# The first feed-forward of a two-layer decoder: seven column blocks accumulated chunk by chunk in whole fp32 products instead of four in split products

## Chip, cores and metric

One NeuronCore of a Trainium2 chip. The metric is the device time of one execution in microseconds. The program is fully unrolled; five engines (PE, DVE, ACT, POOL and SP as DMA queue) work through fixed instruction lists and wait for each other by semaphores.

## Reference

Two decoder layers on 256 tokens of width 1024, every sub-layer with an RMS norm and a shift, scale and gate from the conditioning c. Only the very first sub-layer matters here:

```python
c_act = jax.nn.silu(c)
mod = (c_act @ w_ada[l] + b_ada[l]).reshape(bsz, 3, 3, D_MODEL)
sh, sc, gt = _ada(mod, 0)
h = h + 0.5 * gt * swiglu(modulate(rms_norm(h, norm_g[l, 0]), sh, sc), ffn_w_in[l, 0], ffn_w_out[l, 0])
...
def modulate(x, shift, scale): return x * (1.0 + scale) + shift
def swiglu(x, w_in, w_out):
    g, u = jnp.split(x @ w_in, 2, axis=-1)
    return (jax.nn.silu(g) * u) @ w_out
```

w_in is 1024 x 5632, so x @ w_in has 22 pairs of 128-column blocks (a gate block and an up block); w_out is 2816 x 1024. Everything is float32.

## The kernel before

Activations lie transposed: 8 chunks of 128 features by 256 tokens. An fp32 product is made of three fp32r products (`mm3`, L466 to L468): both operands are split into a high part (a cast to fp32r) and a low part (the rest). A weight block of 1 MB ("w": one pair of column blocks, two halves of 128x1024) goes from HBM into one of four `st` buffers; ACT casts each half to `wh` (L384 or L387) and DVE subtracts to get `wl` (L413). Two of these subtractions, the fourth and the fifth that the program emits (`NLP = [4, 5]` in `low`), are given to POOL. The first eight halves lie in pieces of 512 columns in tiles of the pool `y` (`EX1 = 8`), later ones in `wh` and `wl`. "Sum" below means one such pair of column blocks: two halves x 8 chunks x 3 products = 48 matmuls of 256 columns into one PSUM bank. The first feed-forward's first product has 22 sums.

The conditioning is made by DVE: a block "a" of 1 MB (w_ada) holds shift and scale of one chunk, and two multiply-and-reduce instructions (L393) turn it into two columns of `mod`. `first_input` has a closure `each(k)`: it emits block a of chunk k, the two small DVE operations on it, and on ACT the chunk `uh[k]` = high part and `v` = the whole value in fp32; POOL makes the low part `ul[k]` from the two (L1650) and the next normed chunk (L1631).

So the first feed-forward cannot start before its conditioning. `ORD` says in which order the first blocks are loaded and used: a at an "a", a weight block at a "w". In `ffn`, at an "a" the chunk is applied to all weight halves that are there, at a "w" the new halves are applied to all chunks that are there. The first four sums grow that way. Then `prepare(NPREP)` gets four more halves ready, `act(j)` turns each finished bank into `silu(g) * u` and splits it (ACT L737, DVE L738, ACT L275, DVE L276), `tables()` loads rope tables and gains and lets POOL multiply them out (L1672 to L1692, 39 instructions), and the remaining 18 sums follow one by one. Their halves, and the a blocks of the later sub-layers between them, are emitted by `fill`, which is called from `clk.tick` and asks a planner's clock what would be on time. All of this fixes the order of each engine's list when the program is built; `pin` keeps it.

Of the kernel before, what the change touches and what calls it, by code (L numbers as in the profile page):

```python
# [29 lines left out]
NT = 6  # L30
ORD = 'aaaawawawwaa'
NLP = [4, 5]
# [29 lines left out]
NPREP = 4  # L62
UPTO = 21, 26, 40, 52, 60, 68, 76
P = 128
D = 1024
KC = 8
S = 256
# [156 lines left out]
class _Kernel:  # L224
# [55 lines left out]
    def plan(self):  # L280

        io = self.io
        q = []
# [12 lines left out]
        ffn_in = lambda n: blk("w_in", n * NJ, NJ)  # L296
        ffn_out = lambda n: blk("w_out", n * 11, 11)
        U = UPTO
        ws = ffn_in(0)
        nw = 0  # L300
        for e in ORD:
            q.append(("a", len(q) - nw) if e == "a" else ("w",) + ws[nw])
            nw += e == "w"
        phase(ws[nw:], U[0])
        phase(ffn_out(0), U[1])
        ws = []
# [8 lines left out]
        ws = ffn_in(2)  # L315
# [10 lines left out]
        for j, e in enumerate(q):  # L326
            if j == nsa:
                self.stop = len(self.queue)
            for i in range(2):
                if e[0] == "a" or i * 1024 < e[2]:  # L330
                    self.queue.append((e, i))
# [4 lines left out]
        self.released, self.hold = 0, False  # L336
        self.freed = []
        self.lows = []
        self.lpos, self.issued, self.staged, self.stages = 0, 0, {}, 4
        self.depth, self.slack, self.lag = 6, SG, 0.0  # L340

    def load(self, upto=None):

        clk, sync = self.clk, self.nc.sync
        while self.lpos < len(self.queue) and (upto is None or self.lpos < upto):
            e, i = self.queue[self.lpos]
# [15 lines left out]
            if e[0] == "w":  # L362
                sync.dma_start(out=st[:, 0:e[2]], in_=e[1])
            else:
                sync.dma_start(out=st, in_=self.io["w_ada"][e[1]])
            for _ in range(1 if e[0] == "w" and e[2] == 1024 else 2):
                self.staged[self.lpos] = st, clk.dma + 2000
                self.lpos += 1

    def emit(self):  # L370
# [4 lines left out]
        self.qpos += 1  # L375
        clk = self.clk
        early = e[0] == "a" and e[1] < EARLY
        src = self.st if early else self.st[:, i * 1024:(i + 1) * 1024]
# [344 lines left out]
    def ffn(self, u, gate_fn, prep, each=None):  # L723
# [35 lines left out]
        if each is not None:  # L759
            ks = 0  # L760
            for e in ORD:
                if e == "a":
                    each(ks)
                    if w:
                        outer(ks, range(len(w)))
                    ks += 1
                else:
                    ps.append(self.psmm() if len(ps) < 3 else self.pssc())
                    n = len(w)
                    w += [self.half(n + i > 0) for i in range(2)]  # L770
                    for k in range(ks):
                        outer(k, range(n, n + 2))
            first = len(ps)
        else:
# [9 lines left out]
            for k in range(K1, KC):  # L784
                outer(k, range(2 * first))
        if each is not None:
            self.prepare(NPREP)
        for j in range(first):
            act(j0 + j, ps[j])
        if each is not None:  # L790
            self.tables()
# [824 lines left out]
    def first_input(self):  # L1616
# [7 lines left out]
        nc.scalar.copy(out=rstd, in_=self.rstd)  # L1624
        hn = []

        def norm():
# [9 lines left out]
        def each(k):  # L1637
# [7 lines left out]
            T = clk.on("V", 200)  # L1645
            v = self.tmp((P, S))
            for o in (th[:, k, :], v):
                nc.scalar.activation(out=o, in_=hn[k], func=AF.Identity, bias=sh[:, k:k + 1], scale=gs[:, k:k + 1])
                T = clk.A(2 * S, T)
# [141 lines left out]
def _layout(i):  # L1791
# [18 lines left out]
    wi = i["ffn_w_in"].reshape(4, KC, P, 2, NJ, P).transpose(0, 4, 2, 3, 1, 5)  # L1810
    L["w_in"] = ct(wi).reshape(4 * NJ, P, 2048)
    wo = i["ffn_w_out"].reshape(4, NJ, P, KC, P).transpose(0, 3, 1, 2, 4).reshape(4 * 11, 16, P, P)
    L["w_out"] = ct(wo.transpose(0, 2, 1, 3)).reshape(44, P, 2048)
# [46 lines left out]
```

## Time and profile before

| | |
|---|---|
| time before, median of 3 runs | 1305.77 us (1304.62 to 1307.18) |
| the profiled execution | 1304.5 us; its span 1302.7 us |
| busy in the span | PE 94%, DVE 75%, ACT 50%, POOL 20% |
| first matmul of the first feed-forward | at 24.30 us |
| its first four sums done, next sum starts | 60.37 us |
| first matmul with w_out | 163.18 us |

In the trace every fp32r matmul is one record of MATMUL and one of LDWEIGHTS (row PEld); a plain fp32 matmul leaves two of each. Records of PE overlap, so the distance of starts is the pace and the length of a record is not. PEclk in the views is 1.00 where the throttle granted the full rate; whether TensorE runs at 1.2 or 2.4 GHz is seen from the distance of starts.

### The profile page before, as it was taken

Reading aid. Unit: us, or ns where it says so; the run is one execution under the profiler, and the core shown is the slowest. Engines: PE = TensorE matmul, PEld = TensorE weight load, DVE = VectorE, ACT = ScalarE, POOL = GpSimd, SP = SyncE. Lnnn points to the kernel's source line nnn. Section 1 sums busy time; section 2 is a strip of 40 time slices with the busy share of each in tenths; the row PEclk is TensorE's granted clock in tenths of the full one; section 3 lists DMA queues with packets and bytes.
Section 4 is the critical chain, followed back from the end, with each engine's and each line's share of the span. In section 5 each row is a group of like instructions: output and inputs, shape, how many; then the busy total and the mean of one; then the engine's idle time right before and its main releaser. Section 6 shows DMA issues by size and latency. Waiting matters only on the chain.

```text
span 1302.7 us, 23375 instructions
## 1 busy us (share of the span) xinstructions
PE 1224.2 (94%) x9373; PEld 1146.2 (88%) x9373; DVE 976.3 (75%) x1743; ACT 646.3 (50%) x1126; POOL 255.3 (20%) x356
## 2 busy tenths in 40 slices
PE   4899999789989898899999999999999889999998
PEld 3899999677777687799999999989998778999998
DVE  6788886866768677578888878878778997766652
ACT  4545554434445444456545446545435477654441
POOL 3460010462433525110000100030001353000000
PEclk9999999989999999899999999999999899999999
DMA  8889877534353544245888956776983003466650
GB/s 324 303 300 341 325 302 280 196 148 173 133 203 148 197 134 163 91 163 206 327 321 320 343 208 242 272 276 244 334 311 142 33 2 132 162 257 227 239 198 17
DMA packets 42733, 284.50 MB, mean 218 GB/s; under 512 B 5249, under 2 KB 6273, under 8 KB 9346
## 3 DMA queue, kind: packets, MB, share of 16 engines
q1 hardware_dynamic: 42626, 283.02, 58.8%
q8 instruction: 73, 1.20, 0.4%
q14 instruction: 34, 0.28, 0.1%
HBM read 281.96 MB, written 1.05 MB: 217 GB/s over the span
## 4 chain that ended last, share of the span: by engine, by line
PE 73%; DVE 13%; POOL 8%; ACT 3%; issue 2%; DMA 0%; SPq 0%; ACTq 0%; DVEq 0%; POOLq 0%
PE mm L466 18%; PE mm L467 18%; PE mm L468 18%; PE mm L849 3%; PE mm L850 3%; PE mm L851 3%; DVE wl L413 2%; PE tp L906 2%; POOL y L938 2%; POOL rs_t L581 2%; POOL rs_t L584 2%; POOL rs_y L586 2%; POOL rs_t L585 1%; DVE y L1455 1%; DVE st L393 1%
## 5 line engine op out<-in xcount | busy, mean ns | idle before, releaser
L413 DVE TENSOR_TENSOR wl<-st,wh 128x1024 fp32r<-128x1024 f32 x361 | 436.3, 1234 | 94.4 <-ACT wh L387 94.0
L387 ACT CAST wh<-st 128x1024 fp32r<-128x1024 f32 x361 | 369.4, 1048 | 137.3 <-PE mm L468 45.3
L466 PE MATMUL mm<-uh,wh 128*128 128x256 f32 x1304 | 366.5, 281 | 1.6 <-DVE y L738 1.6
L467 PE MATMUL mm<-uh,wl 128*128 128x256 f32 x1304 | 367.9, 282 | 0.0
L468 PE MATMUL mm<-ul,wh 128*128 128x256 f32 x1304 | 365.0, 280 | 0.0
L468 PEld LDWEIGHTS mm<-ul,wh 128*128 128x128 f32 x1304 | 246.8, 189 | 0.0
L466 PEld LDWEIGHTS mm<-uh,wh 128*128 128x128 f32 x1304 | 244.5, 187 | 1.9 <-DVE y L738 1.8
L467 PEld LDWEIGHTS mm<-uh,wl 128*128 128x128 f32 x1304 | 245.0, 188 | 0.0
L466 PE MATMUL mm<-y,wh 128*128 128x256 f32 x832 | 233.4, 281 | 0.1
L467 PE MATMUL mm<-y,wl 128*128 128x256 f32 x832 | 232.4, 279 | 0.0
L468 PE MATMUL mm<-y,wh 128*128 128x256 f32 x832 | 232.2, 279 | 0.0
L393 DVE CUSTOM_DVE_ANT_0 st<-st,cact 128x1024 f32<-128x1024 f32 x152 | 186.7, 1258 | 0.0
L466 PEld LDWEIGHTS mm<-y,wh 128*128 128x128 f32 x832 | 156.4, 188 | 1.1 <-issue 0.9
L467 PEld LDWEIGHTS mm<-y,wl 128*128 128x128 f32 x832 | 156.4, 188 | 0.0
L468 PEld LDWEIGHTS mm<-y,wh 128*128 128x128 f32 x832 | 156.4, 188 | 0.0
L849 PE MATMUL mm<-wh,uh 128*128 128x512 f32 (+1 forms) x336 | 135.0, 402 | 0.0
L850 PE MATMUL mm<-wl,uh 128*128 128x512 f32 (+1 forms) x336 | 131.0, 390 | 0.1
L851 PE MATMUL mm<-wh,ul 128*128 128x512 f32 (+1 forms) x336 | 130.3, 388 | 0.0
L524 POOL TENSOR_TENSOR y<-y 128x256 f32<-128x256 f32 x20 | 22.8, 1138 | 360.3 <-ACT y L505 360.3
L895 POOL TENSOR_TENSOR y<-y 128x512 f32<-128x512 f32 (+1 forms) x26 | 32.3, 1251 | 265.4 <-DVE y L894 157.5
L737 ACT ACTIVATE y<-mm 128x256 f32<-128x256 f32 x84 | 32.2, 383 | 94.2 <-PE mm L468 94.0
L849 PEld LDWEIGHTS mm<-wh,uh 128*128 128x128 f32 x336 | 66.3, 197 | 14.1 <-issue 1.2
(254 smaller groups left out, 1659.2 us busy)
## 6 DMA issues: line engine op xcount, KB each, us to landing
st<-w_in SPq DMA_DIRECT2D x88, 1024.0 KB, 5.1
st<-w_ada SPq DMA_DIRECT2D x76, 1024.0 KB, 5.7
st<-w_out SPq DMA_DIRECT2D x44, 1024.0 KB, 6.8
st<-w_qk SPq DMA_DIRECT2D x24, 1024.0 KB, 4.8
st<-w_va SPq DMA_DIRECT2D x8, 1024.0 KB, 4.7
st<-w_o SPq DMA_DIRECT2D x8, 1024.0 KB, 4.8
st<-w_vb SPq DMA_DIRECT2D x4, 1024.0 KB, 5.0
st<-w_q SPq DMA_DIRECT2D x4, 1024.0 KB, 6.8
```

The lines of the kernel that those rows point to most:

```text
L387: nc.scalar.copy(out=wh, in_=src)
L393: nc.vector.tensor_tensor_reduce(out=src, in0=src, in1=self.cact, scale=1.0, scalar=0.0, op0=ALU.mult, op1=ALU.add, accum_out=self.mod[:, ...
L413: (self.nc.gpsimd if eng == "G" else self.nc.vector).tensor_tensor(out=o, in0=src[:, c], in1=i.bitcast(F32), op=ALU.subtract)
L466: mm(out=out, lhsT=ah, rhs=bh, start=start, stop=False, **kw)
L467: mm(out=out, lhsT=al, rhs=bh, start=False, stop=False, **kw)
L468: mm(out=out, lhsT=ah, rhs=bl, start=False, stop=stop, **kw)
L581: eng.tensor_tensor(out=t, in0=y, in1=y, op=ALU.mult)
L737: nc.scalar.activation(out=sg, in_=ps[:, 0:S], func=AF.Silu)
L849: mm(out=ps[tt], lhsT=uh[k][:, c], rhs=wh[:, o], start=k == 0, stop=False)
L850: mm(out=ps[tt], lhsT=uh[k][:, c], rhs=wl[:, o], start=False, stop=False)
L851: mm(out=ps[tt], lhsT=ul[k][:, c], rhs=wh[:, o], start=False, stop=k == KC - 1)
L895: (eng or nc.gpsimd).tensor_tensor(out=A, in0=A, in1=B, op=ALU.add)
```

## The change

```diff
-ORD = 'aaaawawawwaa'
+ORD = 'aafafafafafafaff'
+NF = 7
...
@@ plan
-        ws = ffn_in(0)
-        nw = 0
+        seen = {"a": 0, "f": 0}
         for e in ORD:
-            q.append(("a", len(q) - nw) if e == "a" else ("w",) + ws[nw])
-            nw += e == "w"
-        phase(ws[nw:], U[0])
+            q.append((e, seen[e]))
+            seen[e] += 1
+        phase(ffn_in(0)[NF:], U[0])
...
@@ load
+            elif e[0] == "f":
+                sync.dma_start(out=st[:, 0:2 * NF * P], in_=self.io["w_first"][e[1]])
@@ emit
+        if e[0] == "f":
+            self.firsts.append(self.st)
+            self.freed.append(max(clk.now, self.arrival) + 6000)
+            return
@@ ffn
         if each is not None:
-            ks = 0
-            for e in ORD:
...
-                    for k in range(ks):
-                        outer(k, range(n, n + 2))
+            ps = [self.psmm() for _ in range(3)] + [self.pssc() for _ in range(2)] + [self.pst(), self.obank]
+            for k in range(KC):
+                each(k)
+                while len(self.firsts) <= k:
+                    self.emit()
+                for i in range(2 * NF):
+                    nc.tensor.matmul(out=ps[i // 2][:, (i % 2) * S:(i % 2 + 1) * S],
+                                     lhsT=self.firsts[k][:, i * P:(i + 1) * P], rhs=self.exact[k],
+                                     start=k == 0 and i % 2 == 0, stop=k == KC - 1, skip_group_check=True)
+                clk.tick(430 * 2 * NF)
             first = len(ps)
...
-        if each is not None:
-            self.prepare(NPREP)
         for j in range(first):
             act(j0 + j, ps[j])
+            if each is not None and j < 2:
+                self.prepare(2 * j + 2)
         if each is not None:
             self.tables()
@@ first_input
+            self.exact.append(v)
@@ _layout
+    L["w_first"] = ct(wi[0, 0:NF].transpose(3, 1, 0, 2, 4)).reshape(KC, P, 2 * NF * P)
```

Seven of the 22 sums (14 half banks, seven of the eight PSUM banks) are now kept open at once. A block "f" (0.92 MB) holds, for one chunk k, the 128 rows of the first seven pairs of column blocks; it is used as it lands, as stationary operand of 14 plain fp32 matmuls with `exact[k]`, the fp32 value `v`. There is no cast and no subtraction for these weights. The other 15 sums are made as before. `NLP` stays [4, 5].

How the lists of the engines move, at three places. Up to the end of the first feed-forward the lists differ; behind it they are the same on every engine.

**POOL, end of the first sums.** `y<-st,y 128x512 x2` is a low part of a weight half in two pieces; `y<-y 128x512` to `qtab` are the tables. Before:

```order
L1631 TENSOR_TENSOR y<-h,y 128x256
L413 TENSOR_TENSOR y<-st,y 128x512 x2
L1650 TENSOR_TENSOR ul<-y,uh 128x256
L413 TENSOR_TENSOR y<-st,y 128x512 x2
L1650 TENSOR_TENSOR ul<-y,uh 128x256 x2
L1672 TENSOR_SCALAR y<-y 128x512
```

With the change, with numbers and waits (st_377 is the second weight block after the f blocks, st_415 the third):

```order
L421 TENSOR_TENSOR y_447<-st_377,y_443 128x512 [waits DMAHW2_49,DVE_49,Activation_49]
L421 TENSOR_TENSOR y_448<-st_377,y_444 128x512 [waits PE_49,Activation_49]
L1679 TENSOR_SCALAR y_511<-y_511 128x512 [waits DMAHW2_49,DVE_49,PE_49]
L1680 TENSOR_SCALAR y_513<-y_513 128x128 [waits DMAHW3_49,DVE_49]
L1682 TENSOR_TENSOR kcg_527<-y_513 128x64 [waits Pool_49]
L1699 TENSOR_TENSOR shareA_530<-y_507,y_511 128x2x32 [waits DMAHW0_49]
L1699 TENSOR_TENSOR shareA_530<-y_507,y_511 128x2x32 x15
L1699 TENSOR_TENSOR shareC_531<-y_507,y_511 128x2x32 x8
L1699 TENSOR_TENSOR ktab_532<-y_509,y_511 128x2x32 [waits DMAHW1_49]
L1699 TENSOR_TENSOR ktab_532<-y_509,y_511 128x2x32 x7
L1699 TENSOR_TENSOR qtab_529<-y_509,y_513 128x2x32 x4
L421 TENSOR_TENSOR y_698<-st_415,y_661 128x512 [waits DMAHW4_49,PE_49,Activation_49]
```

Before, both low parts of POOL stood ahead of the tables; now one stands ahead of them and the other behind all 39 instructions of them.

**PE, the third sum after the f blocks** (its bank is mm_697; mm_624 is the sum before it), with the change:

```order
L474 MATMUL mm_624<-uh_191,y_444 128x256
L475 MATMUL mm_624<-uh_191,y_448 128x256
L476 MATMUL mm_624<-ul_192,y_444 128x256
L474 MATMUL mm_697<-uh_191,y_661 128x256 [waits DVE_49,Activation_49]
L475 MATMUL mm_697<-uh_191,y_698 128x256 [waits Pool_49]
L476 MATMUL mm_697<-ul_192,y_661 128x256
```

The second matmul of this sum takes y_698, the low part that POOL makes behind the tables.

**SP, the loads of the tables.** Before:

```order
L363 DMA st<-w_in 128x2048 x2
L365 DMA st<-w_ada 128x2048
L363 DMA st<-w_in 128x2048
L1661 DMA y<-rope 128x256 x2
L1663 DMA y<-gains 128x512
```

With the change:

```order
L367 DMA st<-w_first 128x1792 x2
L365 DMA st<-w_in 128x2048 x2
L369 DMA st<-w_ada 128x2048
L365 DMA st<-w_in 128x2048
L369 DMA st<-w_ada 128x2048
L365 DMA st<-w_in 128x2048
L369 DMA st<-w_ada 128x2048
L1668 DMA y<-rope 128x256 x2
L1670 DMA y<-gains 128x512
```

The tables' loads now stand behind the eighth f block and seven blocks more (four w, three a), each of which waits for one of the four `st` buffers.

## Rows read from the trace of the kernel before

**Rows 1.** The page: busy time and share of PE, and the chain of waits by engine.

```profile
PE 1224.2 (94%) x9373; PEld 1146.2 (88%) x9373; DVE 976.3 (75%) x1743; ACT 646.3 (50%) x1126; POOL 255.3 (20%) x356
PE 73%; DVE 13%; POOL 8%; ACT 3%; issue 2%; DMA 0%; SPq 0%; ACTq 0%; DVEq 0%; POOLq 0%
```

**Rows 2.** Busy time by stretch: start to end, length, then PE, PEld, DVE, ACT, POOL busy (and instructions), PEclk, DMA share, GB/s.

```profile
19.10:60.40 41.30, 29.11 (x193) 27.25 (x193) 32.11 (x47) 21.31 (x37) 20.78 (x18) 0.96 0.79 306
60.40:163.20 102.80, 102.80 (x865) 102.80 (x866) 88.19 (x129) 51.53 (x78) 26.41 (x39) 1.00 0.88 321
163.20:222.00 58.80, 58.80 (x507) 58.80 (x506) 45.90 (x66) 29.01 (x41) 5.35 (x5) 1.00 0.79 303
```

**Rows 3.** The chain that ended last, from 14 to 62 us (start, us, what).

```profile
24.28 4.37 DVE y L413 x4
...
40.90 4.17 ACT y L384 x8
...
56.48 3.49 DVE wl L413 x3
59.97 0.35 DVE y L738
60.37 0.38 PE mm L466
```

**Rows 4.** The timeline of PE, single matmuls of the first feed-forward (start, length, engine, line, shapes, idle before and its releaser). 16 records lie between the second and the third row.

```profile
24.30 0.58 PE L466 MATMUL mm<-uh,y 128*128 128x256 f32 x1 [8.32 <-ACT y L384]
...
28.16 0.41 PE L466 MATMUL mm<-uh,y 128*128 128x256 f32 x1
...
31.79 0.41 PE L468 MATMUL mm<-ul,y 128*128 128x256 f32 x1
...
36.13 0.39 PE L467 MATMUL mm<-uh,y 128*128 128x256 f32 x1 [1.59 <-POOL y L413]
...
39.65 0.39 PE L466 MATMUL mm<-uh,y 128*128 128x256 f32 x1
...
58.47 0.28 PE L468 MATMUL sc<-ul,y 128*128 128x256 f32 x1
...
163.18 0.28 PE L466 MATMUL mm<-y,wh 128*128 128x256 f32 x1
```

**Rows 5.** Plain fp32 matmuls, two records each: the broadcast of c (line view: shortest, median, longest ns), four transposes in a row in the timeline and by line in the same 12 us; and two fp32r matmuls of 512 columns with 13 records between them.

```profile
L1598 PE MATMUL mm<-cact,ones x4: 1056/1056/1187, 2.3 to 4.9; 1*128 1x512 f32 x4
...
308.69 1.03 PE L906 MATMUL tp<-ident,y 128*128 128x128 f32 x8
...
L906 PE MATMUL tp<-ident,y x8: 270/272/273, 308.7 to 309.4; 128*128 128x128 f32 x8
...
304.50 0.39 PE L849 MATMUL mm<-wh,uh 128*128 128x512 f32 x1
...
307.76 0.39 PE L851 MATMUL mm<-wh,ul 128*128 128x512 f32 x1
```

**Rows 6.** The timeline of ACT: the fp32 value of the first chunk.

```profile
18.47 0.58 ACT L1648 ACTIVATE y<-y,sh,gs 128x256 f32<-128x256 f32 x1
```

**Rows 7.** DMA issues of the whole run: count, size of one, median us from issue to landing.

```profile
st<-w_in SPq DMA_DIRECT2D x88, 1024.0 KB, 5.1
st<-w_ada SPq DMA_DIRECT2D x76, 1024.0 KB, 5.7
...
y<-gains SPq DMA_DIRECT2D x1, 256.0 KB, 6.7
```

**Rows 8.** DVE's low parts of a half in pieces, its reductions of the a blocks from 60 to 163 us (ns: shortest, median, longest), and ACT's casts of eight pieces.

```profile
L413 DVE TENSOR_TENSOR y<-st,y x12: 678/978/1779, 24.3 to 46.9; 128x512 fp32r<-128x512 f32 x12
...
L393 DVE CUSTOM_DVE_ANT_0 st<-st,cact x26: 1212/1219/1342, 65.4 to 154.9; 128x1024 f32<-128x1024 f32 x26
...
40.80 4.26 ACT L384 CAST y<-st 128x512 fp32r<-128x512 f32 x8
```

**Rows 9.** The timeline of ACT: the table load and the first silu, and the fourth.

```profile
58.18 1.28 ACT L737 ACT_TABLE_LOAD   x1
59.48 0.38 ACT L737 ACTIVATE y<-mm 128x256 f32<-128x256 f32 x1
...
63.62 0.38 ACT L737 ACTIVATE y<-sc 128x256 f32<-128x256 f32 x1
```

**Rows 10.** The timeline of POOL during the tables, and by line the shortest, median and longest ns of a table instruction and of a low part's piece.

```profile
60.74 1.50 POOL L1672 TENSOR_SCALAR y<-y 128x512 f32<-128x512 f32 x1 [5.55 <-DMA y<-gains]
...
63.22 10.07 POOL L1692 TENSOR_TENSOR shareA<-y 128x64 f32<-128x64 f32 x16
73.25 6.40 POOL L1692 TENSOR_TENSOR shareC<-y 128x64 f32<-128x64 f32 x8
79.61 6.40 POOL L1692 TENSOR_TENSOR ktab<-y 128x64 f32<-128x64 f32 x8
85.97 1.34 POOL L1692 TENSOR_TENSOR qtab<-y 128x64 f32<-128x64 f32 x4
...
L1692 POOL TENSOR_TENSOR shareA<-y x16: 314/411/1303, 63.2 to 72.0; 128x64 f32<-128x64 f32 x16
...
L1692 POOL TENSOR_TENSOR qtab<-y x4: 317/320/508, 86.0 to 86.8; 128x64 f32<-128x64 f32 x4
...
L413 POOL TENSOR_TENSOR y<-st,y x4: 1297/1726/2253, 34.4 to 42.9; 128x512 fp32r<-128x512 f32 x4
```

More of the change, by code (lines that the diff above doesn't have):

```diff
@@ L329, in plan @@
             for i in range(2):
-                if e[0] == "a" or i * 1024 < e[2]:
+                if e[0] == "a" or i * 1024 < (1024 if e[0] == "f" else e[2]):
                     self.queue.append((e, i))
@@ L337, in plan @@
         self.freed = []
+        self.firsts = []
         self.lows = []
@@ L363, in load @@
                 sync.dma_start(out=st[:, 0:e[2]], in_=e[1])
+            elif e[0] == "f":
+                sync.dma_start(out=st[:, 0:2 * NF * P], in_=self.io["w_first"][e[1]])
             else:
                 sync.dma_start(out=st, in_=self.io["w_ada"][e[1]])
-            for _ in range(1 if e[0] == "w" and e[2] == 1024 else 2):
+            for _ in range(1 if e[0] == "f" or e[0] == "w" and e[2] == 1024 else 2):
                 self.staged[self.lpos] = st, clk.dma + 2000
@@ L759, in ffn @@
         if each is not None:
-            ks = 0
-            for e in ORD:
[L762 to L770, printed above, removed]
-                    for k in range(ks):
-                        outer(k, range(n, n + 2))
+            ps = [self.psmm() for _ in range(3)] + [self.pssc() for _ in range(2)] + [self.pst(), self.obank]
[8 more added lines that the diff above has]
+                clk.tick(430 * 2 * NF)
             first = len(ps)
@@ L1625, in first_input @@
         hn = []
+        self.exact = []
         def norm():
```

## The prediction, made before the changed kernel was run

> **What bounds the kernel now.** I read the page first: PE is busy 94% of the span, and the chain of waits lies on PE for 73% of it [rows 1]. So time is won only where PE waits, or by giving PE less to do. The busy times by stretch say where it waits near the change: from 19.1 to 60.4 us PE is busy for 29.1 of 41.3 us, and from 60.4 to 163.2 for 102.8 of 102.8 [rows 2]. In that second stretch the reader is to see a full PE beside DVE at 86% and DMA at 0.88. It holds 18 sums of 48 matmuls, so a sum costs 102.8 / 18 = 5.71 us, 0.119 a matmul. The chain shows what the first stretch waits for: casts and low parts of the weights (4.37, 4.17, 3.49 us pieces), and last a DVE multiply that frees a bank [rows 3]. PE's timeline gives the result of that stretch: the first product at 24.30 us, the last of four sums at 58.47, the next sum at 60.37 [rows 3, 4]. Everything after the first product with w_out at 163.18 us keeps its order, so I compute when that matmul starts with the change.
>
> **The sums of the f blocks.** What goes: 192 fp32r matmuls, the casts and low parts of their eight halves, and PE's waits for them. What comes: 8 x 14 products of 256 columns in plain fp32, two records each, 224 records.
> - Start. A product needs `v` of its chunk. The first `v` ends at 18.47 + 0.58 = 19.05 us [rows 6], and the f block has by then been loaded like the block before it. Before, PE started 5.25 us later because it needed a cast and a low part too.
> - Pace. Four fp32 transposes in a row are eight records of 128 columns in 1.03 us, the last of them 0.272 long: (1.03 - 0.272) / 7 = 0.108 apart [rows 5]. Twice the columns make 0.217. The other bound is an fp32r matmul that streams 512 columns, as long a stream: 14 steps in 3.26 us, 0.233 each [rows 5]. I take 0.22, near the first, since that row is of the same type. A chunk is then 28 x 0.22 = 6.16 us, eight are 49.3.
> - Clock. After its idle start PE steps by 3.63 / 17 = 0.213 us for 256 columns (the 1.2 GHz level), against 0.119 later; after the wait at 36.13 it is slow once more until 39.65 [rows 4]. About 4 us at half pace cost 2.0 us (1.5 to 2.5).
> - Nothing else should hold PE here. DVE has two reductions of 1.22 us [rows 8] and two small operations a chunk, 3 us of 6.16. Loads take 5 to 6 us to land [rows 7] and are issued two chunks (12 us) ahead or more: each waits for a buffer that PE or DVE gives back, the latest case being the block a of chunk 5, which waits for chunk 1.
>
> So the seven sums end at T = 19.05 + 49.3 + 2.0 = 70.4 us (69.2 to 73.8). Before, seven sums would have been through at 60.4 + 3 x 5.71 = 77.5. DVE's saved work lies beside PE's and is worth nothing by itself.
>
> **The step to the eighth sum.** Its two halves are loaded at about T - 16 (in the buffer of the last a of the phase, once DVE has read it) and land at T - 11; cast and low part take 2 us each [rows 8] and are done by T - 7. The second block follows at T - 12, its last low part on POOL by T - 2. The bank of the first sum must be free: silu after its last product at T - 5.3 and a table load of 1.28 us [rows 9], but DVE's multiply stands behind the two reductions of a later a block, which I place at T - 2.5 to T. I count 0.5 us of wait; before, the same point cost 1.9 us (58.47 to 60.37) [rows 3, 4], which is the upper bound.
>
> **The low part behind the tables.** This is the term that decides. The tenth sum (third after the f blocks) is due at T + 0.5 + 2 x 5.71 = T + 12.0. Its second matmul takes the fifth low part, which POOL makes, and POOL's list now has all 39 table instructions ahead of it. Before, that low part stood ahead of them, and the tables hid under PE's stretch of 102.8 us at no cost.
> - When the tables start. Their loads wait in SP's queue behind the block that needs PE's last chunk (issued at T), one more a, and for the bank work of the first two sums, whose tiles they reuse; the gains go out at about T + 1.6 and land 6.7 us later [rows 7]: T + 8.3 (T + 6 to T + 10).
> - How long they run. Before, from 60.74 to 87.31, 26.6 us [rows 10]; that is the upper bound. But a single table instruction took between 0.314 and 1.303 us, and the last four, in a gap of DVE, 0.320 in the median [rows 10]: the long ones sat beside DVE instructions of 1.2 to 1.3 us [rows 8]. All free they would take 2.35 (the three instructions ahead) + 36 x 0.32 = 13.9 us: the lower bound.
> - DVE now blocks itself. After the seven banks (a step of (63.62 - 59.48) / 3 = 1.38 us each [rows 9], to T + 9.5), the next bank, two reductions, another bank, six pieces of low parts and two reductions more it reaches, at about T + 22, the multiply of the tenth sum, which PE cannot finish. I count for POOL: 2.35 us to T + 10.6; to T + 13.4 beside reductions three instructions at 0.9; to T + 15.8 beside bank work six at 0.41; to T + 22.3 eight at 0.8; the other 19 free, 6.1 us: T + 28.4. The low part's first piece adds 1.3 (at most 2.25) [rows 10]: T + 29.7.
> - So PE waits 17.5 us (9 to 27) there, and goes on at 1.2 GHz for some 4 us, another 2.0 us, as after its waits of before [rows 4].
>
> The Trainium skill has a rule for the spread of those table instructions: "SBUF — State Buffer", section "Who interferes with whom", states that a DVE instruction with two inputs in SBUF and a POOL instruction that reads SBUF hold a shared port pair exclusively, so that one blocks until the other ends. By that rule the tables run free once DVE is blocked and the wait is the 17.5 us above; by the mean of before (24.2 / 36 = 0.67 us each) it would be 26 and the sum +21. The trace agrees with the rule in that the longest table instruction is as long as a DVE reduction.
>
> Could this wait cost nothing? Behind it PE has no slack: it was full for all of the 102.8 us [rows 2], and loads and casts can run ahead by four buffers and a few halves only.
>
> **The sum.** T 70.4, wait 0.5, 15 sums 85.7, wait for POOL 17.5, cold clock 2.0: 176.1 us for the first w_out matmul, against 163.2: **+12.9 us**. On the profiled execution's 1304.5 us that is 1317.4; the median of the runs is 1.3 above that execution, so 1318.7. All low bounds together: 69.2 + 0.3 + 85.7 + 9.2 + 1.5 = 165.9, +2.7. All high: 73.8 + 1.9 + 85.7 + 27 + 2.5 = 190.9, +27.7.
>
> **Rivals.**
> 1. *The low part is there in time: faster.* Without that wait the w_out stretch starts at 156.6, 6.6 us earlier: 1299. It decides at a wait of 4.6 us (with its cold clock 6.6), so POOL would have to end the tables by T + 15.3. For it: the seven sums do end 7 us earlier than seven sums would have before, a gain that is not in dispute, and tables beside an idle DVE are fast. Against: from T + 8.3 that leaves 7 us for 39 instructions, whose fastest rows need 13.9, and the gains would have to land at T + 1.4, before they are issued. Chance 0.06.
> 2. *The stretch after the wait is no longer PE's.* 13 a blocks now share 15 sums, not 18: DVE has 2 x 1.22 + 2.1 + 0.85 = 5.4 us of 5.71 a sum, and DMA carries 28 blocks of 1.05 MB in 85.7 us, 343 GB/s where it had 321 at a share of 0.88 [rows 2]. With four buffers and 5 to 6 us of landing, half a microsecond on each of 12 sums would be +6: 1325. Against: DVE is still below PE's pace. Chance 0.12.
> 3. *The fp32 phase is slow.* If a chunk's loads came late or the clock stayed low between chunks, T moves up; with all records at 1.2 GHz by 47 us: 1330 to 1365. For: the broadcast of c, 512 columns at the start, takes 1.06 us a record [rows 5], which is the low level. Against: it is alone there, and PE's later unbroken work is at the high level. Chance 0.06.
>
> **How the numbers follow.** The forecast, with its wait between 9 and 27 us, has 0.76. Its bounds reach from 1308 to 1333; all high or all low at once is unlikely, so I keep 1308 to 1331 for it. Rival 2 lies inside; rival 1 and most of rival 3 lie outside, 0.12 with the ends. One microsecond below the forecast's own end, 1307, makes up for a rival 1 that comes halfway. A measurement of this kernel tells about 0.2%, 2.6 us, from no change. Faster: rival 1, 0.06. Same: the lowest end of the forecast, 0.05. Slower: 0.89.
>
> **What would show it.** In the changed profile: PE's first fp32 product near 19 us and records 0.22 apart after some 4 us; the eighth sum near 71 us; in the waits PE (and its weight loads) behind POOL's low part, one wait of 9 to 27 us near 83 us; POOL's tables from about 79 us, slow at first and 0.32 us each at the end; DVE idle behind PE meanwhile; the first w_out matmul near 176 us; everything after it shifted by the same amount. The prediction is wrong if that wait is under 5 us, if PE waits for DMA within the f blocks, or if the shift of the w_out stretch is not the difference of the totals.

## The result: slower by 1.0%

| | before | changed |
|---|---|---|
| median, runs of one comparison | 1305.84 us (1304.62 to 1307.18) | 1320.08 us (1317.53 to 1320.75) |
| ratio, 95% interval | | 1.0102 (1.0088 to 1.0116) |
| profiled execution, its span | 1304.5, 1302.7 us | 1320.27, 1318.5 us |
| eighth sum starts | 77.5 us (60.37 + 3 x 5.71) | 71.32 us |
| first matmul with w_out | 163.18 us | 177.52 us |

Predicted were 1318.7 us (1307 to 1331) and 176.1 us for the w_out matmul. That matmul moves by 14.3 us, and the medians differ by 14.2. The spans of the two profiled executions differ by 15.8: PE's products behind are shifted by 14.3 to 14.4 us up to 485 us of the kernel before, by 15.4 to 16.9 from 568 to 1062 us, and by 15.7 at the end. Such steps are also in the trace of the run with the tables in two parts (8.1, then 11.0, then 9.8 us) and not in that of the run with the low part on DVE, both below. Where they come from is not known. What stands behind the first feed-forward's first product is otherwise only shifted.

### The profile after

The page of the changed kernel, to be laid beside [rows 1]. PE is busy for 8 us more in a span that is 16 us longer; DVE and POOL have no more to do than before.

```profile
PE 1232.6 (93%) x9261; PEld 1148.9 (87%) x9261; DVE 954.9 (72%) x1729; ACT 633.1 (48%) x1112; POOL 244.2 (19%) x356
PE 69%; DVE 13%; POOL 9%; ACT 3%; DMA 3%; issue 2%; SPq 0%; ACTq 0%; DVEq 0%; POOLq 0%
```

Busy time by stretch, the columns of [rows 2]: the fp32 sums, the piece up to the end of the long wait, the rest of the 15 sums and its first 4.4 us alone, the w_out stretch.

```profile
19.08:71.30 52.22, 50.68 (x224) 43.97 (x224) 22.54 (x43) 13.56 (x25) 15.80 (x17) 1.00 0.78 292
71.30:100.60 29.30, 11.74 (x98) 11.54 (x98) 16.25 (x31) 12.09 (x27) 18.82 (x41) 0.79 0.46 170
100.60:176.20 75.60, 75.41 (x612) 74.95 (x613) 57.17 (x85) 30.12 (x46) 1.18 (x1) 0.97 0.84 315
100.60:105.00 4.40, 4.40 (x20) 4.40 (x21) 0.00 (x0) 0.00 (x0) 1.18 (x1) 0.50 0.47 162
176.20:235.60 59.40, 59.40 (x510) 59.36 (x509) 48.88 (x70) 32.09 (x45) 5.30 (x5) 1.00 0.85 323
```

The first row shows PE all but full where it had been busy for 29.11 of 41.30 us; the second shows it busy for 11.74 of 29.30; the third shows it full again, with the granted clock at 0.50 in its first 4.4 us. So the loss is one hole of 17.5 us and the low clock behind it. The 1.00 of the first row does not show that PE starts slowly: the distance of starts does, (23.84 - 19.08) / 12 = 0.40 us for the first twelve records, against 0.216 later. PE's timeline names the hole (start, length, engine, line, shapes, idle before and its releaser). The first four rows are the whole of chunk 0 (28 records in the groups of its seven banks); then come the beginnings of chunks 1 and 2, the last products of chunk 7, the eighth sum, the tenth, and w_out.

```profile
19.08 4.93 PE L774 MATMUL mm<-y,st 128*128 128x256 f32 x12 [3.15 <-ACT y L1655]
23.84 1.89 PE L774 MATMUL sc<-y,st 128*128 128x256 f32 x8
25.57 1.03 PE L774 MATMUL tp<-y,st 128*128 128x256 f32 x4
26.43 1.03 PE L774 MATMUL o<-y,st 128*128 128x256 f32 x4
27.30 2.75 PE L774 MATMUL mm<-y,st 128*128 128x256 f32 x12
...
33.34 2.75 PE L774 MATMUL mm<-y,st 128*128 128x256 f32 x12
...
68.73 1.03 PE L774 MATMUL o<-y,st 128*128 128x256 f32 x4
71.32 0.39 PE L474 MATMUL mm<-uh,y 128*128 128x256 f32 x1 [1.56 <-DVE y L746]
...
100.60 0.58 PE L475 MATMUL mm<-uh,y 128*128 128x256 f32 x1 [17.54 <-POOL y L421]
...
177.52 0.28 PE L474 MATMUL mm<-y,wh 128*128 128x256 f32 x1
```

The tenth sum's second matmul waits for POOL's low part. POOL's timeline shows what stood ahead of it, against [rows 10]; DVE's shows why POOL was fast at the end.

```profile
81.62 1.87 POOL L1679 TENSOR_SCALAR y<-y 128x512 f32<-128x512 f32 x1 [12.92 <-DMA y<-gains]
...
84.46 9.33 POOL L1699 TENSOR_TENSOR shareA<-y 128x64 f32<-128x64 f32 x16
93.75 2.25 POOL L1699 TENSOR_TENSOR shareC<-y 128x64 f32<-128x64 f32 x8
95.97 2.25 POOL L1699 TENSOR_TENSOR ktab<-y 128x64 f32<-128x64 f32 x8
98.18 1.14 POOL L1699 TENSOR_TENSOR qtab<-y 128x64 f32<-128x64 f32 x4
99.29 2.49 POOL L421 TENSOR_TENSOR y<-st,y 128x512 fp32r<-128x512 f32 x2
```

```profile
67.91 1.87 DVE L401 CUSTOM_DVE_ANT_0 st<-st,cact 128x1024 f32<-128x1024 f32 x1 [1.57 <-DMA st<-w_ada]
...
69.71 1.21 DVE L401 CUSTOM_DVE_ANT_0 st<-st,cact 128x1024 f32<-128x1024 f32 x1
70.86 0.08 DVE L401 DVE_READ_ACCUMULATOR2_ANT mod<- 128x1 f32 x1
70.86 0.41 DVE L746 TENSOR_TENSOR y<-y,mm 128x256 f32<-128x256 f32 x1
...
90.90 1.33 DVE L401 CUSTOM_DVE_ANT_0 st<-st,cact 128x1024 f32<-128x1024 f32 x1
92.16 0.08 DVE L401 DVE_READ_ACCUMULATOR2_ANT mod<- 128x1 f32 x1
108.92 0.42 DVE L746 TENSOR_TENSOR y<-y,mm 128x256 f32<-128x256 f32 x1 [16.69 <-ACT y L745]
```

From 92.2 us DVE stands at the multiply of the sum that PE cannot finish. From then on POOL's table instructions follow each other every 0.28 us (8 in 2.22, from 93.75 to 95.97). Eleven of the 16 in the row ahead began before the halt, from 84.46 to 92.37 us, and took 0.72 each. DVE's halt, itself a consequence of POOL's lateness, shortens that lateness.

### The profile page after: what moved, and what is told of

It is laid out like the page before. It is cut to its first block, busy times and chain, and to the rows that moved or that the text cites. A ratio compares the mean times of both kernels' runs of the same rounds, so it can differ in the third digit from the quotient of the medians.

```text
span 1318.5 us, 23125 instructions
## 1 busy us (share of the span) xinstructions
PE 1232.6 (93%) x9261; PEld 1148.9 (87%) x9261; DVE 954.9 (72%) x1729; ACT 633.1 (48%) x1112; POOL 244.2 (19%) x356
## 4 chain that ended last, share of the span: by engine, by line
PE 69%; DVE 13%; POOL 9%; ACT 3%; DMA 3%; issue 2%; SPq 0%; ACTq 0%; DVEq 0%; POOLq 0%
PE mm L474 16%; PE mm L475 16%; PE mm L476 16%; PE mm L854 3%; PE mm L855 3%; DVE wl L421 3%; PE mm L856 3%; PE tp L911 2%; POOL rs_t L589 2%; POOL rs_t L592 2%; POOL y L943 2%; POOL rs_y L594 1%; DMA st<-w_in 1%; POOL rs_t L593 1%; DVE y L1460 1%
## 5 line engine op out<-in xcount | busy, mean ns | idle before, releaser
L421 DVE TENSOR_TENSOR wl<-st,wh 128x1024 fp32r<-128x1024 f32 x347 | 418.3, 1232 | 89.5 <-ACT wh L395 88.9
L395 ACT CAST wh<-st 128x1024 fp32r<-128x1024 f32 x347 | 355.0, 1048 | 131.9 <-PE mm L476 52.7
L475 PE MATMUL mm<-uh,wl 128*128 128x256 f32 x1192 | 336.6, 282 | 0.2 <-DVE wl L421 0.2
L474 PE MATMUL mm<-uh,wh 128*128 128x256 f32 x1192 | 335.0, 281 | 0.0
L476 PE MATMUL mm<-ul,wh 128*128 128x256 f32 x1192 | 333.7, 280 | 0.0
L476 PEld LDWEIGHTS mm<-ul,wh 128*128 128x128 f32 x1192 | 225.6, 189 | 0.0
L475 PEld LDWEIGHTS mm<-uh,wl 128*128 128x128 f32 x1192 | 223.9, 188 | 0.7 <-DVE wl L421 0.6
L474 PEld LDWEIGHTS mm<-uh,wh 128*128 128x128 f32 x1192 | 223.5, 188 | 0.0
```

The costliest lines, as they stand in the source:

```text
L395: nc.scalar.copy(out=wh, in_=src)
L421: (self.nc.gpsimd if eng == "G" else self.nc.vector).tensor_tensor(out=o, in0=src[:, c], in1=i.bitcast(F32), op=ALU.subtract)
L474: mm(out=out, lhsT=ah, rhs=bh, start=start, stop=False, **kw)
L475: mm(out=out, lhsT=al, rhs=bh, start=False, stop=False, **kw)
L476: mm(out=out, lhsT=ah, rhs=bl, start=False, stop=stop, **kw)
```

## The experiments

Theory: the fp32 sums and the earlier start bring some 6 us, and the order of POOL's list, low part behind 39 table instructions, takes 17.5 us and 2 us more at the low clock (called the cold clock below). Rivals: the stretch behind is bound by something else (DVE, transfers), so that without that wait the gain would not show; or the fp32 sums themselves cost. The first four runs share one comparison with the kernel before (1306.89 us), the next four one (1306.87), the next three one (1306.31), the last has 1306.96. Line numbers are those of the changed kernel. Code is shown in parts: "..." stands for lines left out.

The last two columns are read from one profiled execution each, in us: when the first w_out matmul starts, and the rest of the span behind it. The kernel before has 163.18 and 1139.5 there, the changed kernel 177.52 and 1141.0. That execution is not the median one: 1302.29 us with the tables in w_out, 1311.16 with one a block later, 1301.57 with the low parts ahead of the activation.

| run | median us | ratio to before (95%) | first w_out matmul | rest |
|---|---|---|---|---|
| low part on DVE | 1305.29 | 0.999 (0.9981 to 0.9999) | 161.77 | 1140.5 |
| third block ahead of the tables | 1305.55 | 0.9991 (0.9982 to 1.0001) | 162.60 | 1140.8 |
| tables in two parts | 1316.02 | 1.0071 (1.0056 to 1.0086) | 171.22 | 1141.3 |
| before, 13th low part on POOL | 1319.63 | 1.0096 (1.0079 to 1.0113) | 178.17 | 1140.7 |
| third block ahead, tables in w_out | 1304.52 | 0.9986 (0.9977 to 0.9995) | 160.38 | 1140.1 |
| the same, one a block later | 1309.68 | 1.003 (1.0017 to 1.0043) | 161.83 | 1147.5 |
| before, tables in w_out | 1306.12 | 0.9995 (0.9986 to 1.0004) | 163.17 | 1142.7 |
| one a block later, six fp32 sums | 1304.09 | 0.9977 (0.9968 to 0.9986) | 158.52 | 1141.4 |
| four activations later | 1309.28 | 1.0029 (1.0013 to 1.0044) | 161.41 | 1143.7 |
| low parts ahead of the activation | 1305.84 | 1.0005 (0.9988 to 1.0022) | 159.84 | 1139.8 |
| both | 1305.94 | 1.0003 (0.9993 to 1.0013) | 159.50 | 1144.7 |
| seven low parts on POOL | 1311.98 | 1.0043 (1.003 to 1.0057) | 163.50 | 1143.9 |

### The fifth low part on DVE

```
-NLP = [4, 5]
+NLP = [4]
```

> The changed kernel, with only the fourth low part on POOL (NLP = [4]): the fifth goes to DVE, where it stands behind the bank work of the ninth sum. Theory (PE waited 17.5 us, and 2 us more at the low clock, for a low part queued behind POOL's tables): that wait is gone, but DVE cannot start the low part before the ninth sum ends at about 82.8 us; bank work 2.4 us and a piece of 0.65 us leave a wait of 3 to 3.5 us at the tenth sum. Total 1304 (1302 to 1306), 16 us below the changed kernel. Rival A (the tables hold DVE and POOL back whoever makes the low part): 1312 or more. Rival B (the fp32 products themselves are the loss): 1318 to 1321, no change.

Measured: 1305.29 us. The long wait has become one of 3.05 us for DVE's low part, and POOL's tables, with no halted DVE beside them, last from 80.65 to 110.76 us:

```profile
85.18 0.58 PE L475 MATMUL mm<-uh,y 128*128 128x256 f32 x1 [3.05 <-DVE y L421]
...
83.52 12.23 POOL L1699 TENSOR_TENSOR shareA<-y 128x64 f32<-128x64 f32 x16
95.71 5.42 POOL L1699 TENSOR_TENSOR shareC<-y 128x64 f32<-128x64 f32 x8
101.09 6.40 POOL L1699 TENSOR_TENSOR ktab<-y 128x64 f32<-128x64 f32 x8
107.45 3.31 POOL L1699 TENSOR_TENSOR qtab<-y 128x64 f32<-128x64 f32 x4
```

One number in a list gives back all 14 us: the wait is the loss, and the fp32 sums do not cost. The tables take 30.1 us here and 17.7 in the changed kernel, which fits that the wait there was as short as 17.5 us only because DVE was halted. But of the 7.1 us by which the eighth sum starts earlier (70.38 against 77.5) 1.4 us remain at w_out: the wait of 3.05 us and the cold clock behind it, products 0.21 us apart for some 5 us, take the rest.

### The third block prepared ahead of the tables

```
-            if each is not None and j < 2:
+            if each is not None and j < 3:
                 self.prepare(2 * j + 2)
```

> The changed kernel with one number changed in ffn: six halves are made ready within the bank work instead of four (j < 3 instead of j < 2), so POOL's list has both low parts ahead of the tables again. Theory: no wait at the tenth sum, no low clock behind it; the tables hide under PE as before the change. First w_out matmul at 177.5 - 17.5 - 2.0 = 158 us, total 1300 (1298 to 1303), which is 5 to 7 us faster than the kernel before: the gain of the f blocks by itself. Rival A (POOL or DVE is the bound of this stretch): the wait reappears at the next low part or spread over the sums, total above 1308. Rival B (the fp32 products are the loss): 1316 or more.

Measured: 1305.55 us, a miss by 5 us. The long wait is gone here too, with no low part taken off POOL: the tenth sum waits for nothing, the eleventh for 0.49 us. What was not foreseen is in the waits view, columns as it says, from 60 us on:

```profile
engine line waited for: us in total, times, longest us
PE mm L475 <- DVE wl L421: 3.5, 5, 1.3
PE mm L474 <- DVE y L746: 0.9, 1, 0.9
PE mm L475 <- DVE y L421: 0.5, 1, 0.5
```

Five short waits for DVE's low parts, spread over the later sums: 91.7 us for 15 sums that PE alone does in 85.7. That is the size and the place of the prediction's second rival, hidden in the changed kernel by the hole; whether DVE or the loads are behind these waits stays open (below). The reader is to see two things: the second miss of a schedule shows only once the first is repaired, and an estimate "PE's pace from here on" needs a row that shows PE at its pace with this much beside it.

### The tables in two parts

Twenty of the 36 table products moved behind the fifth low part.

```
-            self.tables()
+            later = self.tables()
+            next(later)
+            next(later)
         for j in range(j0 + first, NJ):
+            if each is not None and j == j0 + first + 4:
+                for _ in later:
+                    pass
...
+        yield
         for gi in range(9):
+            if gi == 4:
+                yield
```

`tables` is a generator now; its first piece issues the loads and three instructions, its second the 16 of shareA, and the rest comes ahead of the twelfth sum.

> The changed kernel with POOL's tables split: the three first instructions and the 16 of shareA stay ahead of the low part, the other 20 (shareC, ktab, qtab, 5.64 us in the trace of the changed kernel) come behind it. A dose: theory says the wait at the tenth sum falls by those 5.6 us, from 17.5 to 11.9 us, and the total by the same, to 1314.5 (1313 to 1316). Rival A (the wait is for the tables' loads or for DVE, not for the number of instructions ahead): wait 17 to 18 us, total 1319 to 1321.

Measured: 1316.02 us, at the upper end of what was expected; the wait is 12.01 us (11.9 expected) and w_out starts 6.3 us earlier than in the changed kernel; by the ratios to before the time is 4 us shorter (0.0031 of 1306).

```profile
84.55 9.33 POOL L1707 TENSOR_TENSOR shareA<-y 128x64 f32<-128x64 f32 x16
93.85 2.49 POOL L421 TENSOR_TENSOR y<-st,y 128x512 fp32r<-128x512 f32 x2
95.16 0.58 PE L475 MATMUL mm<-uh,y 128*128 128x256 f32 x1 [12.01 <-POOL y L421]
```

The wait goes by how much stands ahead of the low part in POOL's list: 5.6 us of instructions less (2.25 + 2.25 + 1.14 in the changed kernel), 5.5 us of wait less.

### The kernel before, with a low part behind its tables

```
-NLP = [4, 5]
+NLP = [4, 13]
```

> The kernel before (no f blocks), with the fifth low part back on DVE and the thirteenth given to POOL (NLP = [4, 13]): in POOL's list it stands behind the tables, as in the changed kernel. Theory: the order alone makes the wait. The half is due about 11.4 us after 60.4, at 71.8 us; tables start at about 61 and, with DVE working until it is blocked, end near 80, one piece of 1024 columns adds 2.6 to 3.5 us: PE waits 8 to 13 us plus 2 us at the low clock, total 1315 to 1321. It also loses the wait of 1.6 us that PE had at 36.1 us. Rival (the wait needs the f blocks, their open banks or their loads): 1303 to 1308.

Measured: 1319.63 us, without one plain fp32 product of the change; the wait is 13.16 us, just above the 8 to 13 expected, and w_out starts 15.0 us later than in the kernel before.

```profile
80.74 1.14 POOL L1692 TENSOR_TENSOR qtab<-y 128x64 f32<-128x64 f32 x4
81.84 2.33 POOL L413 TENSOR_TENSOR wl<-st,wh 128x1024 fp32r<-128x1024 f32 x1
84.23 0.58 PE L467 MATMUL mm<-uh,wl 128*128 128x256 f32 x1 [13.16 <-POOL wl L413]
```

So the cause is shown from both sides: taken out of the change the loss goes, put into the kernel before it comes.

### Where the rest of the gain goes: the tables elsewhere, one block later, six sums

The base of these runs is the third block ahead of the tables, with `self.tables()` called after the first w_out sum (d == 0) instead of ahead of the eighth input sum:

```
-        if each is not None:
-            self.tables()
...
             self.residual(d, ps, gate)
+            if each is not None and d == 0:
+                self.tables()
```

> The changed kernel with the third block prepared ahead of the tables, and now the whole preparation of the tables (its loads and its 39 GpSimd instructions) after the first of the eight w_out sums instead of ahead of the eighth input sum. Theory A: what kept the kernel with the third block ahead at 1305.6 instead of 1300 is VectorE in the 15 input sums, and the tables make it slow: its two-input operations took 1.33 us beside them and 1.21 without. Some 25 such operations lie in 81.5 to 113 us, so 25 x 0.12 = 3.0 us come back; the five waits of TensorE for wl low parts (3.5 us) fall to 0.5 or so, the first w_out product comes at 159.6 instead of 162.6, the time is 1302.6 (1301.5 to 1304). Theory B: the a blocks in the list alone bind VectorE and the tables don't matter: 1305.6 (1304.8 to 1306.4), waits as before. Theory C: the tables are in the way in the w_out stretch (of VectorE's low parts or GpSimd's squares there): what is gained ahead of 160 is lost again before 222, 1304.5 to 1307.

One a block later (`UPTO`, how many a blocks are due by the end of each kind of weights, begins with 20 instead of 21):

> As the run with the tables in the w_out stretch, and the number of conditioning blocks that are due by the end of the input weights is 20 instead of 21, so that one block (two reductions of 1.22 us on VectorE, 1.05 MB) goes behind them. Theory A (VectorE binds the 15 sums): 1 to 2 us less than that run, 1301.2 (1300 to 1303). Theory B (VectorE has slack once the tables are gone): no change against it, within 0.7 us.

The kernel before with the tables in the same place:

> The kernel before with the tables moved behind the first of the eight w_out sums, nothing else. TensorE is busy 102.80 of 102.80 us in 60.4 to 163.2 there, so VectorE's slower operations beside the tables cost it nothing and their removal gives nothing: 1305.8 (1305 to 1306.5) by theory A and B. If moving the tables is worth something by itself, for instance since their loads meet less traffic, it shows here: 1303 or less.

One a block later and six fp32 sums (`NF = 6`, one bank less in `ps`):

> As the run with one conditioning block later, and 6 sums instead of 7 (12 products a chunk, 768 KB of w_first instead of 896) in the fp32 stretch. If that stretch goes by TensorE's pace: a chunk is 12 x 0.433 + 0.1 = 5.3 us instead of 6.16, the stretch ends 7 us earlier, one sum more in three passes takes 5.71: 1.3 us less than that run, 1300 (1298.5 to 1301.5). If the conditioning's own pace (5.16 us a chunk in the kernel before, with its a blocks and loads) becomes the bound, or VectorE with two more low parts and three fewer microseconds, the gain is gone: 1301 to 1304, with waits of TensorE for ACT's y in the fp32 stretch or for DVE's wl behind it.

Measured: 1304.52, 1309.68, 1306.12 and 1304.09 us. Only the third is what both theories A and B said: moving the tables is worth nothing in the kernel before.

With the third block ahead, moving them brings w_out to 160.38 instead of 162.60 us, VectorE's reductions take 1.22 us again, and the five waits are 2.6 us instead of 3.5. So theory A (contention with the tables) had the right sign; the medians differ by 1.0 us, not 3, and the intervals of the two runs overlap. The time lies at the edge of theory C's range (1304.5 to 1307), but its mechanism is not there: of the 2.8 us by which the first w_out matmul comes ahead of the kernel before, 2.2 are left at the end of that stretch.

The run with one a block later fits neither theory by its time, but its total says nothing of the 15 sums: with 22 reductions in them instead of 24 they take 90.48 us against 90.12, no change, as theory B had it. Its loss lies behind them: PE waits 2.43 us for a low part at 170.25 us, in the w_out stretch, and 2.41 us for ACT at 231.15, with slow products behind.

Six sums in fp32 has the lowest median of the study, 2.8 us below before (its interval overlaps that of the seven sums). In its 16 sums little is left of the waits for low parts:

```profile
PE mm L474 <- DVE y L746: 2.7, 1, 2.7
PE mm L475 <- DVE wl L421: 0.7, 1, 0.7
```

But the loss has only moved. Its fp32 sums end at 62.04 us, as PE's pace said; then comes the wait of 2.7 us for the first bank, with a cold clock behind it. 16 sums of 5.71 us from 62.04 would end at 153.4 us; w_out starts at 158.52, 5.1 us later. With seven sums and the tables in w_out the fp32 sums end at 69.26, 15 sums would end at 154.9, and w_out starts at 160.38, 5.4 us later. Nor does the conditioning's share explain it: the traces have the reductions of 13 a blocks in the 18 sums of the kernel before (0.72 a sum), of 11.5 in 16 with six fp32 sums (0.72), of 12 in 15 with the tables in w_out (0.80) and of 11 in 15 with one a block later (0.73), and this last one is no faster in its 15 sums.

### The order in VectorE's list

In the run with the tables in w_out VectorE stood idle for 1.46 us at 132.5 and 1.77 us at 152.2 us, at the multiply of a sum that PE had just ended, with the low parts that PE then needed behind it. Two edits, alone and together: of the seven activations only three at once, the others two after each following sum; and from the eighth sum on both low parts of the next block ahead of the activation.

```
-        for j in range(first):
+        pend = [(j0 + j, ps[j]) for j in range(first)]
+        for j in range(3 if each is not None else first):
-            act(j0 + j, ps[j])
+            act(*pend.pop(0))
...
-            act(j, ps)
+            pend.append((j, ps))
+            for _ in range(min(2, len(pend))):
+                act(*pend.pop(0))
```

```
+            if each is not None and j < NJ - 1:
+                self.prepare(2)
             act(j, ps)
```

> The kernel with the third block ahead and the tables in the w_out stretch (1304.5), and of the seven activations behind the fp32 stretch only three at once: the other four, whose banks nobody waits for, go two after each of the following sums. Theory D (the reserve is lost in 71 to 85 us): there the seven activations fill VectorE's list, whose reductions and low parts stand behind them, so the four st buffers stay full, SP issues no load from 77.4 to 87.1 us, and the sums later meet late weights: five waits for wl low parts, 2.6 us, and 1.8 us in slower products, 90.1 us for 15 sums that are 85.7 at full pace. With four activations out of the way the loads go on at 75 to 80 us, and 3 to 4 us come back: the first w_out product at 157 instead of 160.4, 1301 (1299.5 to 1302.5). Theory E (the conditioning blocks' share is too high over all 15 sums, 13 blocks in 15 sums against 13 in 18 before): the waits only move, 1304 (1303 to 1305).

> The kernel with the third block ahead and the tables in the w_out stretch, and from the eighth sum on both low parts of the next block stand in VectorE's list ahead of the activation of the sum just done. Theory F (order alone: VectorE stood idle for 1.46 us at 132.5 and 1.77 at 152.2 in that activation's multiply, with the low parts that TensorE waited for behind it): the waits for wl fall from 2.6 us to under 1, 1302.5 (1301.5 to 1303.5). Theory D or E (late loads; the weights' copies on ACT waited 4.17 us for the w_in transfer at 130.2): no change, 1304.5 (1303.5 to 1306), the same waits, now with VectorE waiting for ACT's wh instead of y.

> Both edits of the two runs beside it. Theory D: as with the four activations later, 1301, and not more than 1 us better. Theory F: 1301 to 1302, most of it already in the run with the low parts ahead. Theory E: 1304 in all three.

Measured: 1309.28, 1305.84 and 1305.94 us. None is a gain on 1304.52. Theory D fell: an a block went out sooner (82.55 instead of 87.11 us), and the DMA share from 80 to 90 us is 0.64 instead of 0.31, but from 90 to 100 us it is 0.55 instead of 0.95, and w_out starts 1.0 us later. Besides, PE now waits 1.0 us at 88.93 us for one of the banks that nobody was to wait for. Most of the 5 us in the median of this kernel lies behind the first w_out matmul (1143.7 us of rest against 1140.1). Theory F took 0.5 us off the start of w_out and 0.7 off the waits, and nothing off the median; the twelve times of that kernel reach from 1301.35 to 1312.91 us, so a microsecond or two could not be told by them. Theory E named 1303 to 1305 for all three, and none lies there.

### Seven low parts on POOL

```
-NLP = [4, 5]
+NLP = [4, 5, 10, 13, 16, 19, 22, 25, 28]
```

> The kernel with the third block ahead and the tables in the w_out stretch (1304.5), and 7 of the 24 low parts that are made in the stretch of the 15 sums (the 10th, 13th, ... 28th in number) on GpSimd, which has nothing to do there from 77 to 160 us. What is left after the three runs before is theory E: VectorE's work for a sum is two low parts (2.4 us), 13/15 of two reductions (2.1), the activation's two operations (0.85) and the gap of 0.47 between these, 5.8 us against TensorE's 5.71, so that no order of its list makes room. Seven low parts less are 8.5 us in 90; a low part on GpSimd took 2.6 to 3.0 us there, and VectorE's two-input operations 1.33 instead of 1.21 beside GpSimd, which takes back 16 x 0.12 = 1.9. Theory E: the waits for wl (2.6 us) and most of the 1.8 us of slower products go, the first w_out product at 157 instead of 160.4, 1301.3 (1300 to 1303). If it is the weights' arrival (four st buffers, transfers) that binds, and not VectorE: the waits stay or grow, now for POOL too, 1304 to 1307.

Measured: 1311.98 us, a miss by over 10 us. VectorE was not relieved. Rows of DVE, then of POOL, in that kernel:

```profile
93.08 3.40 DVE L401 CUSTOM_DVE_ANT_0 st<-st,cact 128x1024 f32<-128x1024 f32 x1
...
107.93 3.41 DVE L401 CUSTOM_DVE_ANT_0 st<-st,cact 128x1024 f32<-128x1024 f32 x1
...
131.53 3.42 DVE L401 CUSTOM_DVE_ANT_0 st<-st,cact 128x1024 f32<-128x1024 f32 x1
```

```profile
92.34 3.06 POOL L421 TENSOR_TENSOR wl<-st,wh 128x1024 fp32r<-128x1024 f32 x1 [14.26 <-ACT wh L395]
107.45 2.81 POOL L421 TENSOR_TENSOR wl<-st,wh 128x1024 fp32r<-128x1024 f32 x1 [12.05 <-ACT wh L395]
...
130.86 3.00 POOL L421 TENSOR_TENSOR wl<-st,wh 128x1024 fp32r<-128x1024 f32 x1 [6.12 <-ACT wh L395]
```

A reduction that starts behind a POOL low part ends 1.1 us after that low part: 107.45 + 2.81 = 110.26, 107.93 + 3.41 = 111.34. It takes 3.4 us instead of 1.22, as if it could do nearly all of its work only when POOL was done. Four reductions paid 2.2 us each, and three other operations of VectorE 0.5 to 1.3: about 11.7 us lost for 7 x 1.22 = 8.5 saved. The expectation had charged 0.12 us an operation, the price beside the short table instructions. The 15 sums take 91.94 us instead of 90.12, and 3.8 us more are lost behind the first w_out matmul. So this run does not tell whether VectorE binds the 15 sums; it tells that these subtractions on POOL do not relieve it. The expectation also counted 13 a blocks beside the 15 sums where the trace has 12; with 12 its 5.8 us of VectorE's work a sum are 5.7, no more than TensorE's pace.

What stays open: which of VectorE's work, the weights' arrival and the order of the lists costs the 15 sums their last 4 us (90.1 us from 70.26 to 160.38 with the tables in w_out, against 85.7). Leaving out the a blocks' reductions alone, with their loads kept, would tell the first two apart; it was not tried. One lead is in the traces: with the tables in w_out the DMA share falls to 0.31 from 80 to 90 us, where the kernel before has 0.75, and is 0.88 from 100 to 158 us (0.91 before), so there is little room to make that up.

## Why the prediction held, step by step

- **The fp32 sums.** Start 19.08 us (19.05 said). Pace: chunk 1 begins at 27.30 and chunk 2 at 33.34, 6.04 us for 28 records, 0.216 each (0.22 said, bounds 0.217 to 0.233). Chunk 0 took 8.22 (27.30 - 19.08), so the slow start cost 2.2 (2.0 said). The last product ends at 69.76 (T = 70.4 said). Nothing else held PE there, so the third rival is out.
- **The step to the eighth sum.** The wait was 1.56 us, not 0.5: the multiply that frees the bank stood behind two reductions, as said, and they began at 67.91 as said, when their block had landed; but the fp32 sums ended 0.6 us earlier than said, and the first reduction took 1.87 instead of 1.22 us beside POOL's fourth low part. So the two ended at 70.86, 1.1 us after the fp32 sums. The upper bound of 1.9 held. The sum starts at 71.32 (70.9 said).
- **The wait for the low part.** 17.54 us, 17.5 said, from three terms of which two were off and cancelled; that it agrees to 0.1 us is luck. The tables began at 81.62, 2.9 us later than said and, at 11.9 us after the last fp32 product, outside the 6 to 10 stated: the gains went out at 72.39 and took 9.2 us to POOL's start, not 6.7. They ran 17.7 us instead of 20.1, since the stretch beside VectorE's list was shorter by then. A free table instruction was counted at 0.32 us, the length of its record; the distance of starts is 0.28. VectorE halted at 92.2, said 92.4. That self-made halt is the term that set the size, and it was foreseen: by the mean of the kernel before the wait would have been 26 us, and the run with the low part on VectorE shows tables of 30.1 us when nothing halts it.
- The Trainium skill, "SBUF — State Buffer", section "Who interferes with whom", says that a VectorE instruction with two SBUF inputs and a GpSimd one that reads SBUF lock each other out. Its rule was the reason to count a short end, and the traces agree: 0.28 us a table instruction with VectorE halted, 0.8 (6.40 / 8) with VectorE at work in the run with the low part on it, and the reductions of 3.4 us above.
- **The 15 sums.** 177.52 - 71.32 - 17.54 = 88.66 us, of which 2.0 are the cold clock (products 0.213 us apart from 100.97 to 105.03, granted clock 0.50): 86.7, against 85.7 said. The clock term was right; the pace was 1.0 us short, and 0.6 of it are two waits of PE's weight loads for VectorE's low parts. The prediction put 13 a blocks beside these sums; the trace has 12, since the reductions at 67.91 and 69.71 us are the thirteenth's.
- **The sum.** +14.3 us at the first w_out matmul, +12.9 said: 0.4 from the eighth sum, 1.0 from the 15 sums. Behind it the shift is the same up to the last w_out products (240.0 against 225.5) and on to 485 us; the medians agree with it (14.2), the two profiled spans (15.8) only within the steps told above.
- **The rivals.** The first (low part in time) is out for this kernel, and the run with the third block ahead of the tables, where it is in time, took 1305.55 us, not 1299: there the second rival's +6 comes instead. That rival was given 0.12 for the changed kernel, and there at most 1.0 us of it shows: while PE stands still, the others work on until they block too (the last load goes out at 83.72 us, VectorE halts at 92.2). Without the hole it takes most of the gain.

## What to carry over

When a change removes a reason to make something early, look at what each in-order queue now has ahead of it: here the cheapest engine, 19% busy, held a 1.2 us piece behind 17.7 us of work with no hurry, and the piece was due first. Work that hides under a full engine hides only as long as nothing urgent stands behind it in the same queue. And a stretch that "runs at PE's pace" has that pace only with the load it had; count the other engines' work per step again before a saved microsecond is booked. Last, read a variant at more than one mark: in four of the twelve runs the rest of the span behind the first w_out matmul is 4 us or more longer than in the kernel before, and by their totals alone that would have been put down to the 15 sums.

## Of the hardware, not expected

- A plain fp32 product of 128x128 by 256 columns took 2 x 0.216 = 0.43 us at the 2.4 GHz level, where three fp32r products took 3 x 0.119 = 0.36. The whole-fp32 form is the slower one on TensorE by a fifth; it won only the time in which PE had waited for casts and low parts. The Trainium skill, "FP8 and Floating Point Precision", section "TensorE Precision Notes", counts four passes for true fp32. The trace is near it: 0.43 us is 3.6 times the 0.119 us between fp32r products.
- Contention of VectorE and POOL has two prices. Beside 64-column table instructions a VectorE operation of 1024 columns took 1.33 instead of 1.22 us. When it started inside a 1024-column POOL subtraction, four reductions took 3.4.
